# Decay tiles from a transpose and two-row products, block inverses on 128 partitions, four splits left out, and a new order

## The chip, the cores and the metric

One Trainium2 chip, one of its cores. The time is the device time of one execution in microseconds (us); the kernel before takes 655.69 us, the median of 3 runs (655.58 to 655.97).

## What is computed

The reference is one decoder layer on 512 rows of 1024 float32 numbers. A modulated normalisation feeds one input projection; half of its columns go to a gated delta rule with 4 heads, half to a sparse attention; both meet in an output projection, and a gated MLP with a short convolution follows. The change lies in the gated delta rule, in what leads up to it, and in the order of everything:

```python
gc = jnp.cumsum(g, axis=-1)
decay = jnp.exp(jnp.where(incl, gc[..., :, None] - gc[..., None, :], NEG_INF))
a_mat = jnp.where(strict, jnp.einsum('bhncd,bhnsd->bhncs', k_beta, k) * decay, 0.0)
t_mat = lax.linalg.triangular_solve(eye + a_mat, jnp.broadcast_to(eye, a_mat.shape),
                                    left_side=True, lower=True, unit_diagonal=True)
...
u = t_mat @ (v * beta[..., None])
w = t_mat @ (k_beta * jnp.exp(gc)[..., None])
...
xs = tuple(jnp.moveaxis(t, 2, 0) for t in (u, w, q_dec, k_dec, attn_intra, g_last))
_, o = lax.scan(step, state0, xs)
```

The reference takes chunks of 64 rows; the kernel takes 4 chunks of 128, with the same result.

## The kernel before, in words

The program is written as a long list of operations, in sections: filling matmuls at the start (`warm`, as many as `IDLE` says), normalisation and modulation of the input, the first projection (`g0`, over 8 slices k of the contraction), small gate projections (`small`), convolutions, norms, the delta rule, the attention, the output projection, and the MLP (`up1`, `down`). The first of the delta rule's sections are `prep`, `blocks`, `invert` and `scan`. While the list is written, `record` only notes each operation with the tiles that it touches. Then `emit` issues all of them, some 7,000, in an order that a packed table in the file (`ORDER`) fixes, and a second table (`CHOICE`) says for those that either ScalarE (ACT) or VectorE (DVE) could do which of them does it. Each engine works through its own part of the list in that order, and waits where an operand isn't ready or a buffer not free. Buffers are taken from fixed classes as the list goes: 90 of 512 columns (S), 4 of 1024 columns for raw loads (R), 32 small ones (s), 8 PSUM banks (P), and kept ones (C). So the table sets which buffer is reused when, too. All instructions are issued by one line of `emit`, which is why the profile shows one line for all of them: L280 before, L273 after.

Matrix products are done in float32 accuracy by splitting each operand into a rounded high part and a low part (`split`), and by three passes: high x high, high x low, low x high. Weights come from DRAM as raw loads on the sync engine's queue (SP); some of the accumulating transfers go through GpSimd's (POOL).

For the delta rule, `prep(t)` makes for each of the 4 chunks the tile exp(decay) for all 4 heads at once: VectorE multiplies the log decays by a triangle (`tg`), splits the product, and TensorE sums a mask (`negTr`) and the two halves over 128 rows with a matrix of ones (`onesr`) into the PSUM bank `pb`; ScalarE takes the exponential. The strictly triangular matrix times decay, `uu`, goes to DRAM (`du`).

`blocks` fetches the 64 diagonal blocks of 32x32 from there (4 chunks x 4 heads x 4 blocks), one block on each of 64 partitions, in two halves of 16 rows (`uh`), and inverts all of them at once by forward substitution: in 31 steps VectorE multiplies a column of the block by a row of the inverse so far, and subtracts that from the rows below. The inverse lies in two halves too (`xh`), so most steps take three instructions. It is written to DRAM (`dx`), and `invert(t)` fetches it back with one row a partition (`xc`), spreads it to a block diagonal matrix (`xx`), and joins blocks of 32 to 64 and to 128 by products on TensorE.

`norm2` normalises the input of the MLP, and splits it into `h2h` and `h2l`, some columns of which nobody reads.

## Time and profile before

| | us |
|---|---|
| median of 3 runs | 655.69 |
| span of the profiled execution | 653.6 |
| TensorE (PE) busy, 4,170 instructions | 647.5 |
| VectorE (DVE) busy | 623.9 |
| ScalarE (ACT) busy | 471.8 |
| GpSimd (POOL) busy | 135.5 |
| the 16 DMA engines, mean | 202 GB/s over the span |

The profiled execution has no time of its own beside its span; the median of the runs is 2.1 us above it. The table shows busy time, which counts an instruction from its start to its end; those of one engine overlap, so the price of one in a full queue is the distance from start to start.

### The profile page before, as it was taken

The page shows a single profiled execution, that of the slowest core. Times are in us where ns is not written, and L with a number is a line of the kernel's source. Part 1 is how long each engine was busy: PE and PEld are TensorE (multiplying, and loading weights), DVE is VectorE, ACT ScalarE, POOL GpSimd, SP SyncE. Part 2 cuts the span into 40 slices and gives each one's busy share as a digit, 9 for nine tenths or more (in the row PEclk, how much of TensorE's full clock was granted, in tenths as well). Part 3 has the DMA queues.
Part 4 walks back from the last instruction along what each step waited for, and adds up shares of the span by engine and source line. Part 5 has one row for each costly group of instructions (what it writes and reads, how often), then busy time and mean ns, then how long its engine had stood idle before and what let it go on. Part 6 is the DMA issues. An engine that isn't in the chain of part 4 may idle for free.

```text
span 653.6 us, 12682 instructions
## 1 busy us (share of the span) xinstructions
PE 647.5 (99%) x4170; PEld 584.0 (89%) x4170; DVE 623.9 (95%) x1542; ACT 471.8 (72%) x1184; POOL 135.5 (21%) x158
## 2 busy tenths in 40 slices
PE   9999999999999999999999999999999999999997
PEld 9886888888988889888899999999999998888886
DVE  7999999989999999999999999999989999999997
ACT  6666996355679998746875665766677899998850
POOL 0000100010100003302222523334234432344400
PEclk9999999999999999999999999999999999999999
DMA  9997656656524689985777998999899999999913
GB/s 321 393 357 260 193 184 191 195 136 171 136 66 131 195 275 243 230 255 128 174 157 195 174 178 191 218 218 197 204 226 211 202 235 268 274 182 205 152 30 130
DMA packets 67484, 132.03 MB, mean 202 GB/s; under 512 B 11333, under 2 KB 11989, under 8 KB 67417
## 3 DMA queue, kind: packets, MB, share of 16 engines
q1 hardware_dynamic: 45352, 91.07, 41.6%
q0 software_dynamic: 22064, 40.14, 37.1%
q8 instruction: 33, 0.54, 0.3%
q14 instruction: 35, 0.28, 0.1%
HBM read 109.42 MB, written 3.41 MB: 173 GB/s over the span
## 4 chain that ended last, share of the span: by engine, by line
PE 89%; DVE 5%; DMA 4%; issue 1%; ACT 1%; SPq 0%; DVEq 0%
PE P L280 89%; DVE S L280 4%; DMA R<-in_wg_dram 2%; DMA S<-in_adat_dram 2%; DMA S<-in_x_dram 1%; ACT S L280 1%; SPq L280 0%; DVE C L280 0%; DVE s L280 0%; DVEq L280 0%
## 5 line engine op out<-in xcount | busy, mean ns | idle before, releaser
L280 PE MATMUL P<-S,S 128*128 128x256 f32 (+4 forms) x3675 | 604.1, 324 | 0.0
L280 PEld LDWEIGHTS P<-S,S 128*128 128x128 f32 (+2 forms) x3675 | 522.0, 190 | 53.4 <-issue 0.4
L280 DVE TENSOR_TENSOR S<-S,S 128x512 fp32r<-128x512 f32 (+14 forms) x489 | 245.0, 545 | 6.0 <-ACT S L280 2.0
L280 ACT ACTIVATE S<-S 128x512 fp32r<-128x512 f32 (+3 forms) x378 | 187.5, 548 | 41.0 <-DVE S L280 28.6
L280 ACT ACTIVATE S<-P 128x256 f32<-128x256 f32 (+4 forms) x208 | 83.4, 420 | 64.6 <-PE P L280 61.3
L280 POOL DMA_DIRECT2D S<-R x46 | 43.3, 971 | 289.2 <-DVE S L280 158.6
L280 ACT ACTIVATE S<-R 128x512 fp32r<-128x512 f32 (+2 forms) x153 | 85.9, 583 | 18.7 <-DMA R<-in_wn_dram 6.0
L280 POOL DMA_DIRECT2D S<-in_wu_dram x66 | 62.8, 1017 | 134.7 <-DVE S L280 97.9
L280 DVE SCALAR_TENSOR_TENSOR S<-S,C,S 128x511 f32<-128x511 f32 (+2 forms) x116 | 85.0, 744 | 0.8 <-ACT S L280 0.6
L280 DVE TENSOR_TENSOR S<-P,S 128x256 f32<-128x256 f32 (+3 forms) x124 | 65.3, 535 | 7.6 <-PE P L280 5.0
L280 DVE TENSOR_TENSOR S<-R,S 128x512 fp32r<-128x512 f32 (+2 forms) x100 | 57.6, 588 | 0.4 <-ACT S L280 0.3
L280 ACT ACTIVATE S<-S,C 128x512 f32<-128x512 f32 (+1 forms) x70 | 44.9, 657 | 15.6 <-DVE S L280 7.7
L280 PE MATMUL P<-C,S 128*128 128x128 f32 (+2 forms) x285 | 51.1, 268 | 0.6 <-DVE S L280 0.5
L280 PEld LDWEIGHTS P<-C,S 128*128 128x128 f32 (+1 forms) x285 | 36.8, 145 | 7.5 <-DVE S L280 0.9
L280 DVE SCALAR_TENSOR_TENSOR S<-S,S 128x512 f32<-128x512 f32 x62 | 40.9, 685 | 1.0 <-DMA S<-in_adat_dram 1.0
L280 ACT ACTIVATE S<-S,s 128x128 f32<-128x128 f32 (+4 forms) x75 | 34.3, 479 | 4.2 <-DVE s L280 4.1
L280 ACT ACTIVATE S<-P,C 128x128 f32<-128x128 f32 (+1 forms) x71 | 28.0, 436 | 10.9 <-PE P L280 8.1
L280 POOL DMA_DIRECT2D S<-S x24 | 21.1, 892 | 51.0 <-ACT S L280 46.2
L280 DVE SCALAR_TENSOR_TENSOR S<-P,C,S 128x511 f32<-128x511 f32 (+3 forms) x48 | 29.9, 643 | 0.2
L280 ACT ACTIVATE S<-P,C,C 128x128 f32<-128x128 f32 (+2 forms) x35 | 16.6, 530 | 9.4 <-DVE C L280 8.3
L280 DVE TENSOR_TENSOR S<-S,P 128x256 f32<-128x256 f32 (+1 forms) x39 | 18.6, 477 | 0.6 <-PE P L280 0.4
L280 PE MATMUL P<-S 128*128 128x256 f32 (+1 forms) x96 | 17.3, 322 | 1.2 <-DVE S L280 1.2
(79 smaller groups left out, 296.8 us busy)
## 6 DMA issues: line engine op xcount, KB each, us to landing
S<-in_wu_dram POOLq DMA_DIRECT2D x66, 256.0 KB, 5.7
S<-in_adat_dram SPq DMA_DIRECT2D x64, 256.0 KB
S<-R POOLq DMA_DIRECT2D x46, 256.0 KB, 5.7
S<-in_wu_dram SPq DMA_DIRECT2D x44, 256.0 KB
R<-in_wu_dram SPq DMA_DIRECT2D x22, 512.0 KB
S<-in_wd_dram SPq DMA_DIRECT2D x44, 256.0 KB
S<-in_adag_dram SPq DMA_DIRECT2D x32, 256.0 KB
R<-in_wn_dram SPq DMA_DIRECT2D x12, 512.0 KB
```

Source lines behind the costliest of these rows:

```text
L280: getattr(engines[eng], method)(*map(place, args), **{k: place(v) for k, v in kw.items()})
```

## The change

- `prep`: the log decays, which lie as columns, are turned into rows once, by one transpose on TensorE into the bank `pgr`; the 16 rows are split, and two small transfers on GpSimd's queue lay them out as `grow`, with the high and the low row of each chunk on two neighbouring partitions. The second and third pass into `pb` become one, over two rows. The triangle product, its split and their buffers go. This adds the chunk's row to the exponent without the triangle; the column's part is the exponential's bias, as before, and the mask still closes the upper half.
- `blocks`: the inverse's even columns lie on partitions 0 to 63 and its odd ones on 64 to 127. The blocks are copied to the upper 64 partitions by two more transfers, each step takes one product and one difference over half as many columns, and the two memsets go. The result is written to `dx` with even and odd columns interleaved again by rows of 16, `2048x1x16`, twice; `invert` reads it as before and spreads it in two instructions instead of one.
- `norm2`: four splits whose result nobody reads are left out (t = 3, kk up to 3).
- `IDLE` is 57 instead of 64, the constant `eye16` is replaced by `eye2` (256 columns more), and a function that nothing calls, `up_mm`, is gone.
- `ORDER` and `CHOICE` are new for the whole program.

```diff
-IDLE = 64
+IDLE = 57
...
+    pgr, gcf = bank("pgr"), u("gcf", F32R, (P, 256))[:16]
+    T.transpose(pgr[:16, :P], gc, ident)
+    split(pgr[:16, :P], gcf[:, :P], gcf[:, P:])
+    grow = u("grow", F32R)
+    for i in range(2):
+        G.dma_start(bass.AP(tensor=grow.tensor, offset=grow.offset + i * 512, ap=[[32 * 512, 4], [P, 4], [1, P]]),
+                    gcf[:, i * P:i * P + P])
+
     def prep(t):
         tok = toks[t]
         pb = bank("pb")
-        tg, gh_, gl_ = u("tg"), u("gh", F32R), u("gl", F32R)
-        V.tensor_mul(h4(tg), rows4(cs("triu")), bc(g[:, t * 4:t * 4 + 4]))
-        split(tg, gh_, gl_)
         T.matmul(h4(pb), identr, rows4(negTr), start=True, stop=False)
-        T.matmul(pb, onesr, gh_, start=False, stop=False)
-        T.matmul(pb, onesr, gl_, start=False, stop=True)
+        T.matmul(pb, onesr[32 * t:32 * t + 2, :], grow[32 * t:32 * t + 2, :], start=False, stop=True)
...
-        uh = [u("ub", shape=(P, 16, 32))[:64] for _ in range(2)]
-        xh = [u("xb", shape=(P, 16, 32))[:64] for _ in range(2)]
+        uh = [u("ub", shape=(P, 16, 32)) for _ in range(2)]
+        xb = u("xb", shape=(P, 32, 16))
...
-        tm = u("r")[:64]
-        eye = cs("eye16")[:64].rearrange("p (i j) -> p i j", i=16)
         for i in range(2):
-            V.memset(xh[i], 0.0)
-            V.tensor_copy(xh[i][:, :, i * 16:i * 16 + 16], eye)
+            Q.dma_start(uh[i][64:], uh[i][:64])
+        tm = u("r")
+        V.tensor_copy(xb, cs("eye2").rearrange("p (i j) -> p i j", i=32))
         for j in range(31):
-            n, m = 31 - j, j + 1
+            n, m = 31 - j, j // 2 + 1
...
-            top = max(0, 15 - j)
-            if top:
-                V.tensor_sub(xh[0][:, j + 1:16, 0:m], xh[0][:, j + 1:16, 0:m], tv[:, :top, :])
-            lo = max(0, j - 15)
-            V.tensor_sub(xh[1][:, lo:16, 0:m], xh[1][:, lo:16, 0:m], tv[:, top:, :])
-        for i in range(2):
-            Q.dma_start(dx[:, i * 512:(i + 1) * 512], xh[i].rearrange("p i j -> p (i j)"))
+            V.tensor_sub(xb[:, j + 1:32, 0:m], xb[:, j + 1:32, 0:m], tv)
+        for s in range(2):
+            Q.dma_start(dx.rearrange("p (i s j) -> p i s j", i=32, s=2)[:, :, s, :], xb[s * 64:s * 64 + 64])
...
-                if t % 2:
+                if t == 1 or t == 3 and kk > 3:
...
+c-nQFcbHVw()DYf?w%QjAtOl6QF6{mybL+RfaIW(gXA0)BuZ2yBN8M_lB^OWNJer7LCG*o=svr?-<kV9-(T;0dE^e==j>g(YSpT>`t*p@k^P!X>dIby7aoW=
...
```

What the new order moves is shown at three places. The first is TensorE's beginning. Before, its queue begins as follows; S_79 is the filler's operand and P_141 its bank, C_117 the identity, and the passes of 128x1 are sums over partitions:

```order
L280 MATMUL P_141<-S_79 128x256 x29
L280 MATMUL P_171<-C_117,C_115 128x128 x4
L280 MATMUL P_180<-C_117,C_115 128x128 x4
L280 MATMUL P_141<-S_79 128x256 x7
L280 MATMUL P_198<-C_117,S_83 128x128
L280 MATMUL P_141<-S_79 128x256 x2
L280 MATMUL P_211<-C_117,S_83 128x128
L280 MATMUL P_141<-S_79 128x256 x7
L280 MATMUL P_222<-C_115,S_213 128x1
L280 MATMUL P_141<-S_79 128x256
L280 MATMUL P_222<-C_115,S_213 128x1
```

After, S_85 and P_103 are the filler's:

```order
L273 MATMUL P_103<-S_85 128x256 x13
L273 MATMUL P_117<-C_90,C_81 128x128
L273 MATMUL P_119<-C_90,C_81 128x128 x2
L273 MATMUL P_117<-C_90,C_81 128x128 x2
L273 MATMUL P_119<-C_90,C_81 128x128 x2
L273 MATMUL P_117<-C_90,C_81 128x128
L273 MATMUL P_103<-S_85 128x256 x14
L273 MATMUL P_189<-C_90,S_83 128x128
L273 MATMUL P_191<-C_90,S_83 128x128
L273 MATMUL P_197<-C_90,S_83 128x128
L273 MATMUL P_103<-S_85 128x256 x11
L273 MATMUL P_197<-C_90,S_96 128x128
```

A run of 29 fillers has become one of 13, ahead of the eight small passes that make the modulation's columns; the transposes of the input (C_90 against S) and the sums over partitions stand in larger groups. Behind these rows, 39 passes of the projection's first slice stand ahead of the second slice before, and 42 after.

The second place is the load queue SP, around the second slice of the projection's weights (`in_wg_dram`, the second in each list). Before:

```order
L280 DMA S_200<-in_adat_dram 128x512
L280 DMA S_213<-in_adat_dram 128x512
L280 DMA R_259<-in_wg_dram 128x896
L280 DMA S_263<-in_adat_dram 128x512
L280 DMA S_280<-in_adat_dram 128x512
L280 DMA S_283<-in_adat_dram 128x512
L280 DMA S_285<-in_adat_dram 128x512
L280 DMA S_301<-in_adat_dram 128x512
L280 DMA S_303<-in_adat_dram 128x512
L280 DMA S_317<-in_adat_dram 128x512
L280 DMA S_321<-in_adat_dram 128x512
L280 DMA R_326<-in_wg_dram 128x896
```

After:

```order
L273 DMA S_173<-in_adat_dram 128x512
L273 DMA S_201<-in_adat_dram 128x512
L273 DMA S_206<-in_adat_dram 128x512
L273 DMA S_221<-in_adat_dram 128x512
L273 DMA S_237<-in_adat_dram 128x512
L273 DMA S_241<-in_adat_dram 128x512
L273 DMA S_251<-in_adat_dram 128x512
L273 DMA S_258<-in_adat_dram 128x512
L273 DMA S_269<-in_adat_dram 128x512
L273 DMA S_292<-in_ws_dram 128x160
L273 DMA S_302<-in_adat_dram 128x512
L273 DMA R_312<-in_wg_dram 128x896
```

The second slice has moved from place 21 of the queue to place 23: one more load of modulation weights (`in_adat_dram`, 256 KB each) and the small gate projection's weights (`in_ws_dram`, 80 KB) stand ahead of it.

The third place is SP and VectorE around the way of the inverses through DRAM. SP before:

```order
L280 DMA dx<-S_89 64x512
L280 DMA R_1901<-in_wn_dram 128x1024
L280 DMA S_1910<-in_cst_dram 128x195
L280 DMA S_1952<-in_adat_dram 128x512
L280 DMA S_1962<-in_adat_dram 128x512
L280 DMA dx<-S_87 64x512
L280 DMA S_2006<-dx 128x4x32
L280 DMA S_2008<-in_adat_dram 128x512
L280 DMA S_2056<-dx 128x4x32
```

SP after:

```order
L273 DMA dx<-S_1187 2048x1x16
L273 DMA S_1798<-in_adat_dram 128x512
L273 DMA R_1811<-in_wt_dram 128x1024
L273 DMA dx<-S_1187 2048x1x16
L273 DMA S_1861<-in_adat_dram 128x512
L273 DMA S_1869<-dx 128x4x32
L273 DMA S_1876<-dx 128x4x32
L273 DMA R_1878<-in_wn_dram 128x1024
L273 DMA S_1888<-in_adat_dram 128x512
L273 DMA S_1901<-dx 128x4x32
```

VectorE after, the last rows ahead of and with the first spreading of the inverse (S_1869 is `xc`):

```order
L273 SCALAR_TENSOR_TENSOR S_1823,s_1822<-S_1295,S_245 128x512
L273 TENSOR_TENSOR S_1796<-S_1796,C_79 128x512
L273 SCALAR_TENSOR_TENSOR S_1830,s_1829<-S_1263,S_245 128x512
L273 SCALAR_TENSOR_TENSOR S_1836,s_1835<-S_1686,S_245 128x512
L273 SCALAR_TENSOR_TENSOR S_1838,s_1822<-S_1251,S_255 128x512
L273 TENSOR_SCALAR C_1841<-C_1646 128x16
L273 SCALAR_TENSOR_TENSOR S_1844,s_1843<-S_955,S_255 128x512
L273 SCALAR_TENSOR_TENSOR S_1854,s_1853<-S_1189,S_245 128x512
L273 SCALAR_TENSOR_TENSOR S_1866,s_1843<-S_971,S_245 128x512
L273 TENSOR_TENSOR S_1874<-R_1693,S_1757 128x512
L273 SCALAR_TENSOR_TENSOR S_1886,s_1885<-S_1713,S_255 128x512
L273 TENSOR_TENSOR S_1890<-S_1869,S_1764 128x256 x2
```

The second write of `dx` now stands behind a raw load (R_1811, 512 KB), which goes into a buffer that VectorE frees with the difference from R_1288, four rows ahead of the first of these; ten rows of the modulation's products, and four others of that length or shorter, stand between that and the inverse's first multiply.

More of the change, by code (lines that the diff above doesn't have):

```diff
@@ new lines @@
+Vx*01Q}6%(w?D-sOqPfDjQ{VyBIGAkZT$b=^~*YqmP9?ML*=#>mKS<iGfH_msV_90{Hqzb=5Ng`DJ7SD`G4+VWR^VE(`t3D4AR{4k48#5S@geNe^mNw9o9GU
+vFy;4l288Btnx;S%kNrAE@>+HO{>UTeZx<EWeR^^(h^csZgTDS|FdFmX&@8z5B*h!@=7YH$h&L!sku1vP_sxBCkknOXSW+Bxuu4z)JEK!U0!Jl?oKP!<e>JH
+g8#>PMvB!(8Ya<_M@q;QR(7PVY}RWUB=0`SLN+dQ!i?+{CjDf$Zq@u!UCyabCdx8R)Q4JHZs=H|m`euV=~a!8GMu9TwFv4lEh6vv`5!9rA$L91kL5bqPD2hW
+%K+*zMn-Yk#WI8y<5V1DpXe(+tE1!;wF@Idj(j8Sx%*#D;L5j}To%bvP0hM5G?P5xweD2<5xc+Sl;PB{Skl>CJx?B{NG~#xN#gan2BZg>_sJ*nonBOz>n>^q
+d89d{gKX3TT9CVLX*S6$2_VDOIQCL@dB#2mh&9Mh*EA<_Hk8tGmW=#L?ms4Txv0*2Fck%=?o-?6WF`gK59fY|Rqv6{>l&}Mc_*kRwG?YaN@3oK1|!ADUM4Vk
@@ new lines @@
+?A(D|eujq{&7EB&Id^*s{h+os*>JztbdkJ6yUmq{yzV{gsqD=_l+74sNGm4iKzgVPY#N}#hH4L?I(w47fgDNRpAttL>{Aw>as))ZC&n3gqRPbk4h7p1%<R=H
+bZi#qvK}XfzTlvt+^`Ky<)q&V^47{tBt9+boJCvLK-DiNmyXoIo4iHG&O~Wv=G8Z>l8YXWB(pc@o}*fgNs?Sn;L0p}ejzROzleRQE68w79Lqvp{|A-Yj*3i!
+7oQPBP8`7u`n{4I(C_Krp=jLsRCk0-rRVOV!@7g%j`9Q7FQsnT=|azUX5e%$;r@lX2D~)IdtAYX&H$(L=;yR(%fGadMwwue*9b@r>UV*Yc;ByWB28d{5oE-H
+Yop+Uy{zW_=1p#9!+Pn)-*NDL4ltP=6`w*bgWU461m>zQ-fw=yqB6$1b)D)kU3WMsOirn%ek(|JeZpO#q|fM{kdv!gmu}wSj&gi5$?fi-INg!Xef6H#7Lj4@
+Am@q3=rt7636LIzg1_PYu8W>Ti5BL>b;)ccP`cD@??j9DtoO9G)(0?UaY+vA4F#D^>GcG<z)5<_JX}04mW@|j^?u{W!$~9xDLm=>0{;&$X8o@
@@ L181 @@
 """
 CHOICE = """
[L183 to L185 removed]
+c-qBLu?@mN3_L%H6j6OiLGdLeBfKI8$Ox2-VMQ#E4Ja9fk`WjM;`e_(37`~6oRnC$le6y(M0gay7C(Vm_Sr6k3qZ}hyAGky=L2}0T3~g%&+A5ZvNG}7l7sQ7
+M;Q~xY>Z|`C^##@L-T#=97E{3!)x#<R?9ZBP|2Jx9ko&~bu&z;<n4f3O`TZl-B<tRcP7q7`CbYIp``4p--K-(d^Dy?J4h`%gu`$jokhZzZ8-JP3kgj{q=L<>
+RVcWT6U)GOf3N@G2{9iOVg
@@ L739, in invert @@
         xx, yy = u("X"), u("Y")
-        V.tensor_mul(xx.rearrange("p (h b j) -> p h b j", h=4, b=4),
-                     xc.rearrange("p h (o j) -> p h o j", o=1).to_broadcast([P, 4, 4, 32]),
-                     cs("bd").rearrange("p (o b q) -> p o b q", o=1, q=1).to_broadcast([P, 4, 4, 32]))
+        xc = xc.rearrange("p h (s j) -> p h s j", s=2)
+        for s in range(2):
+            V.tensor_mul(xx.rearrange("p (h b j s) -> p h b j s", h=4, b=4, s=2)[:, :, :, :, s],
+                         xc[:, :, s, :].rearrange("p h (o j) -> p h o j", o=1).to_broadcast([P, 4, 4, 16]),
+                         cs("bd").rearrange("p (o b q) -> p o b q", o=1, q=1).to_broadcast([P, 4, 4, 16]))
         V.transpose(yy, xx)
@@ L1128, in hybrid_block @@
     act = [None] * NF
-    def up_mm(ps, wc, a, b):
-        for k in range(KT):
-            mm3(ps[:, a:b], cols(wc[k // 4], hs[k % 4]), (h2h[k][:, a:b], h2l[k][:, a:b]), k == 0, k == KT - 1)
     def conv3(ps, f, s):
```

229 lines of the change are left out of this document (104 added, 125 removed).

## The prediction

> **What bounds the kernel now.** I read the page's head and its chain first, then the chain in order of time.
>
> ```profile
> span 653.6 us, 12682 instructions
> PE 89%; DVE 5%; DMA 4%; issue 1%; ACT 1%; SPq 0%; DVEq 0%
> ```
>
> ```profile
> 6.75 5.92 DMA S<-in_adat_dram
> 12.69 6.93 DMA R<-in_wg_dram
> 19.64 5.87 DMA S<-in_adat_dram
> ...
> 60.99 0.76 DVE S L280
> 61.80 181.31 PE P L280 x1028
> ...
> 646.15 2.57 DVE S L280 x5
> 648.74 1.11 DVE S L280 x2
> 649.88 0.42 DVE S L280
> ```
>
> The columns are start, length, and what ran. Up to about 32 us the chain follows loads, then VectorE to 61.8; from there it is TensorE's own queue almost to the end, and a tail of about 7 us on VectorE and the store that the change leaves as it is. The span is 653.6 and the median of the runs 655.69, so 2.1 us lie around the span; I add them back at the end.
>
> How full TensorE is, stage by stage, is in the table of windows (busy time and starts of each engine, granted clock, DMA share, GB/s):
>
> ```profile
> core 0: us, PE busy (x) PEld busy (x) DVE busy (x) ACT busy (x) POOL busy (x), PEclk, DMA share, GB/s
> 6.05:16.03 9.98, 9.98 (x87) 9.87 (x87) 9.24 (x50) 8.13 (x20) 0.00 (x0) 1.00 1.03 384
> 16.03:20.70 4.67, 4.67 (x41) 4.67 (x40) 4.67 (x17) 3.73 (x8) 0.00 (x0) 1.00 1.04 391
> 20.70:62.00 41.30, 40.75 (x191) 31.32 (x190) 40.48 (x107) 24.96 (x42) 0.00 (x0) 1.00 0.91 334
> 116.80:143.70 26.90, 26.90 (x132) 22.20 (x132) 24.98 (x88) 13.89 (x31) 2.58 (x3) 1.00 0.56 163
> 340.00:380.00 40.00, 40.00 (x334) 39.91 (x334) 39.14 (x79) 27.72 (x58) 14.43 (x16) 1.00 0.89 190
> 560.00:600.00 40.00, 40.00 (x178) 33.14 (x177) 40.00 (x92) 36.89 (x83) 15.75 (x18) 1.00 0.98 203
> ```
>
> Busy time and length agree in every row but one: between 20.70 and 62.00 TensorE is idle for 0.55 us. So time taken from VectorE or ScalarE is worth nothing by itself: only TensorE instructions that go, and waits of TensorE, count. Two prices come from here: 40.00/334 = 0.120 us from start to start where nearly all matmuls have 256 columns, and 40.00/178 = 0.225 us where nearly all have 512. The start is different: up to 20.7 us the DMA engines are full (share 1.03 to 1.04, 384 to 391 GB/s), and TensorE is kept busy with idle-filling matmuls.
>
> **The change, part by part.**
>
> *The start: seven filling matmuls fewer, new load order: +0.35 us.* The fillers are worth 7 x 0.120 = 0.84 us, but they stand where TensorE waits for data. The first projection matmul is at 16.03:
>
> ```profile
> 16.03 1.24 PE L280 MATMUL P<-S,S 128*128 128x256 f32 x9
> 61.00 0.27 PE L280 MATMUL P<-C,S 128*128 128x128 f32 x1
> 61.80 0.44 PE L280 MATMUL P<-C,S 40*128 40x40 f32 x4 [0.53 <-DVE S L280]
> ```
>
> It needs the first quarter of the normalised input, and in both orders the last load for that is the 14th, behind the same 3.7 MB; so I keep 16.0. Next is the second slice of the projection weights. It was issued at 12.69 and landed 6.93 later at 19.62, and its first use was at 20.70. In the new order it is load 23 instead of 21, with 262 + 82 KB more ahead: 0.344 MB at 391 GB/s is 0.88 us, so it lands at 20.50. ScalarE splits half a slice in 0.53 us (two in 1.05):
>
> ```profile
> 19.64 1.05 ACT L280 ACTIVATE S<-R 128x384 fp32r<-128x384 f32 x2
> ```
>
> That gives 21.03. TensorE itself has 42 first-slice matmuls ahead now (39 before): 16.03 + 42 x 0.120 = 21.07. Both say 21.05, +0.35. Bounds: -0.5, if filler and loads give way together, and +0.9, if the load's whole delay counts.
>
> *TensorE's work behind that point: -1.15 us.* Three of the 256-column matmuls moved ahead of the point, -0.36. Each of the four decay tiles takes two passes of 512 columns instead of three, -4 x 0.225 = -0.90; that the second contracts two rows instead of 128 I price at nothing, since fewer rows have not made passes shorter here:
>
> ```profile
> L280 PE MATMUL P<-S,S 128*128 128x512 f32 x1257 | 319.0, 399 | 0.0
> L280 PE MATMUL P<-S,S 128*40 128x512 f32 x8 | 3.1, 393 | 0.0
> L280 PE MATMUL P<-C,S 40*128 40x40 f32 x4 | 0.4, 236 | 0.5 <-DVE S L280 0.5
> ```
>
> The transpose that makes the rows adds one pass like the last row's, 0.44/4 = 0.11. The new order also changes how often fp32 and rounded passes alternate; no row prices that, and the 0.120 and 0.225 contain it as it was, so it stays at 0, with 0.5 us to either side.
>
> *The wait at 61: -0.6 us.* From 61.00 to 61.80 TensorE starts nothing, where such a pass takes 0.11: 0.69 us lost to VectorE, which was behind (40.48 of 41.30 us busy in that window). Its two memsets are gone, the small gate projection's weights are loaded ahead of the second slice now, and that projection's transposes stand elsewhere. What is late next are the evictions of the gate and norm work at 72 to 78; I leave 0.1 us for them. Bounds: -0.7 and +0.5, a new wait as long as the old.
>
> *The block inverses and the split of the rows on VectorE and ScalarE: 0.* The inverse loop is these rows:
>
> ```profile
> L280 DVE TENSOR_TENSOR S<-S,S 64x192 f32<-64x192 f32 (+23 forms) x78 | 22.4, 301 | 1.9
> ```
>
> 93 small instructions become 62, with half the elements a partition. At 301 ns as a latency, and less from start to start, some 9 us leave VectorE. They lie beside TensorE's 26.90 busy of 26.90 us in that window, so nothing is gained; and were the loop not shorter at all, nothing is lost. The same holds for four splits of 128x256 that nobody reads.
>
> *The inverses' way through DRAM: 0, if pieces of 64 bytes are cheap.* The result was written as rows of 2 KB, and is now written as 2 x 2048 pieces of 64 bytes, then read as before. The trace has pieces of 128 bytes in the reads (512 for 64 KB):
>
> ```profile
> 134.39 0.51 SPq L280 DMA_DIRECT2D dx<-S  x1
> 134.99 0.53 SPq L280 DMA_DIRECT2D R<-in_wn_dram  x1
> ...
> 149.63 0.39 SPq L280 DMA_DIRECT2D S<-dx  x1
> ```
>
> ```profile
> 136.40:137.40 1.00, 1.00 (x6) 0.74 (x5) 0.90 (x4) 0.44 (x1) 0.00 (x0) 1.00 0.76 135
> 150.60:151.30 0.70, 0.70 (x4) 0.58 (x4) 0.70 (x4) 0.52 (x2) 0.00 (x0) 1.00 0.78 117
> ```
>
> 0.78 x 0.70 us x 16 engines / 512 is at most 17 ns a piece, and the read is in by about 151.5, 1.9 after its issue. The write and the weight load behind it were through by about 137.4, so a write takes at most 3.0. In the new order the second write stands behind a 512 KB load into a buffer that VectorE frees; from there to the inverse's first multiply VectorE has 14 more rows, one short and 13 of the length of these two, some 0.61 from start to start, together 8.1 us:
>
> ```profile
> 152.85 0.69 DVE L280 SCALAR_TENSOR_TENSOR S<-S,S 128x512 f32<-128x512 f32 x1
> ...
> 153.47 0.69 DVE L280 SCALAR_TENSOR_TENSOR S<-S,S 128x512 f32<-128x512 f32 x1
> ```
>
> The transfers need three issues of 0.4, 3.0 for the write, 1.8 for its pieces (128 an engine x 17 ns, less the 0.34 that 128 KB took), and 1.9 for the read: 7.9 us. TensorE has 48 passes of 512 columns ahead of the inverse, 10.8 us from the matmul that frees that buffer, and VectorE's chain reaches it after 0.4 + 0.6 + 8.1 + 0.8 = 9.9. So about 1 us is free on both sides; up to some 25 ns a piece it costs nothing. The upper end is a piece as dear as one of 2 KB, 85 ns at 24 GB/s an engine: 128 x (85 - 25) = 7.7 us. I take 0, since the 17 ns row is the nearest.
>
> *The rows' way to the decay tiles: 0.* Two small transfers from GpSimd now feed them, behind a 256 KB accumulation in its queue:
>
> ```profile
> S<-R POOLq DMA_DIRECT2D x46, 256.0 KB, 5.7
> C<-in_par_dram POOLq DMA_DIRECT2D x1, 24.0 KB, 3.3
> ```
>
> Issues of about 0.9 each and 3.3 to 5.7 to land make 5 to 8 us behind the split; between the transpose and the first decay tile TensorE's order has about 10 us of other matmuls. Bounds 0 and +2.
>
> **Sum:** 0.35 - 1.15 - 0.6 = -1.4. 653.6 - 1.4 = 652.2, and with the 2.1 around it 654.3.
>
> **Rivals.** A difference of 0.2%, 1.3 us, is about what can be told from no change.
>
> *The gain is larger.* The start gives back 0.5 instead of taking 0.35, and the alternation is worth 0.5: -1.15 - 0.6 - 1.0 gives 652.9. For it: 4 us of fillers stand ahead of 16.03 in all. Against it: the DMA engines are full there.
>
> *Nothing to measure.* The second slice's delay counts in full (+0.9) and the wait at 61 comes back elsewhere (-0.1): 655.3. For it: VectorE stays the second busiest engine (40.48 of 41.30), and any order of 7,000 rows has places as tight as the one removed. Against it: VectorE has less to do throughout.
>
> *A written piece costs twice a read one.* At 34 ns TensorE waits (34 - 25) x 128 = 1.2 us ahead of the first inverse: 655.5. For it: no write below 2 KB stands in this trace. Against it: nothing but the 17 ns of the reads. The Trainium skill's page "DMA: Bandwidth & Descriptors" (section "Specifications") says that transfers below 512 bytes are read, modified and written back; the reads of 128 bytes to SBUF here show no such price, and for writes to DRAM by that rule the time would be this rival's, or more.
>
> *Slower, by the 64-byte writes.* TensorE stands right behind the first inverse, with the 1 us of margin worked out above. From 25 ns a piece on, each 10 ns cost 1.3 us; slower than before by 1.3 needs 46 ns, and 85 ns gives 662. For it: the chain is serial, and TensorE waits there directly. Against it: 17 ns for reads twice the size.
>
> *It does not relieve VectorE,* because small instructions have a floor. Then the loop still falls by its 31 missing instructions, and TensorE does not notice: 654.3 as well.
>
> **How the numbers follow.** Forecast 654.3 with its near neighbours 0.54 (two thirds of that below 654.4, since the sum's open ends reach further down than up), which holds the loop that relieves nobody; larger gain 0.10; nothing to measure 0.16; doubled pieces 0.06; slower by writes 0.10; by the rows' transfers or a tight place in the attention stage 0.04. Faster by over 0.2%: 0.36 + 0.10 = 0.46. Within 0.2%: 0.18 + 0.16 + 0.06 = 0.40. Slower: 0.14. The range leaves out the far half of the larger gain and most of the slow cases: 652.8 to 657.0.
>
> **What would show it.** Right: the first projection matmul at about 16.0, the first of the second slice at about 21.0; no wait above 0.3 us at 61; TensorE with 4,160 starts and no idle time from 62 to the tail; the loop on VectorE near 13 us with TensorE full beside it; the first inverse's passes without a wait. Wrong: a wait of TensorE ahead of that inverse that ends with the read from DRAM, a projection start away from 16.0, or waits on the decay tiles that end with GpSimd's transfers.

## The result, and the profile after

The changed kernel takes 661.78 us, the median of 6 runs (658.99 to 664.50); the kernel before took 655.83 beside it (655.52 to 656.45, 6 runs). The ratio is 1.0095, with a 95% interval of 1.0076 to 1.0115: slower, outside the range of the prediction and on its other side. The profiled execution took 660.93, 2.1 us more than its span. The page's head, its chain, and the chain in order of time (start, length, what ran):

```profile
span 658.8 us, 12659 instructions
PE 89%; DMA 4%; ACT 3%; DVE 2%; issue 1%; SPq 0%; ACTq 0%; DVEq 0%; POOLq 0%
```

```profile
17.11 44.46 PE P L273 x230
...
67.60 1.28 ACT L273
68.90 0.64 ACT S L273
69.58 78.69 PE P L273 x401
148.28 289.64 PE P L273 x2021
...
440.30 7.23 DMA S<-R
447.57 37.04 PE P L273 x306
```

VectorE has gone from 5% of the chain to 2%, as the change meant it to. But the first projection matmul stands at 17.11 instead of 16.03, TensorE's queue is broken at 68, where before it was not, and from 440 on, in the MLP, DMAs are in the chain, which ran through there on TensorE alone before (start and length again):

```profile
246.62 399.50 PE P L280 x2764
```

None of the three stands at the decay tiles or the inverses, where the diff edits the computation; the diff also takes seven fillers from the start. Whether the new order made these places is what the experiments ask. How TensorE and the DMA engines stood in the MLP, before (first row) and after, is in the table of windows (busy time and starts of TensorE, granted clock, DMA share, GB/s):

```profile
430.00:560.00 130.00, 130.00 (x1024) 1.00 0.99 226
```

```profile
430.00:560.00 130.00, 127.52 (x1011) 1.00 0.96 210
560.00:640.00 80.00, 80.00 (x357) 1.00 0.86 180
```

TensorE stood still for 2.48 us there. The DMA engines were nearly full in both kernels (0.99 and 0.96), but after moved (226 - 210) x 130 = 2.1 MB less, and had to move it later (180 GB/s behind 560, where before had 151). ScalarE's waits in that stretch (us in total, times, longest) show what is late; the same view of before has no such row:

```profile
ACT S L273 <- DMA R<-in_wu_dram: 5.9, 2, 4.4
ACT S L273 <- DMA S<-in_wd_dram: 2.4, 3, 1.5
```

### The profile page after: what moved, and what is told of

Read it like the earlier page. It is cut to its first block, busy times and chain, and to the rows that moved or that the text cites. A ratio compares the mean times of both kernels' runs of the same rounds, so it can differ in the third digit from the quotient of the medians.

```text
span 658.8 us, 12659 instructions
## 1 busy us (share of the span) xinstructions
PE 649.1 (99%) x4160; PEld 582.0 (88%) x4160; DVE 618.6 (94%) x1542; ACT 468.5 (71%) x1158; POOL 138.9 (21%) x160
## 4 chain that ended last, share of the span: by engine, by line
PE 89%; DMA 4%; ACT 3%; DVE 2%; issue 1%; SPq 0%; ACTq 0%; DVEq 0%; POOLq 0%
PE P L273 89%; ACT S L273 3%; DVE S L273 2%; DMA R<-in_wu_dram 1%; DMA S<-R 1%; DMA S<-in_wd_dram 1%; DMA S<-in_x_dram 1%; DVE s L273 0%; ACT L273 0%; SPq L273 0%; ACT s L273 0%; ACT C L273 0%; ACTq L273 0%; DVEq L273 0%; POOLq L273 0%
## 5 line engine op out<-in xcount | busy, mean ns | idle before, releaser
L273 PE MATMUL P<-S,S 128*128 128x256 f32 (+3 forms) x3675 | 605.6, 323 | 2.6 <-ACT S L273 2.1
L273 PEld LDWEIGHTS P<-S,S 128*128 128x128 f32 (+1 forms) x3675 | 524.2, 189 | 58.8 <-ACT S L273 4.6
L273 DVE TENSOR_TENSOR S<-S,S 128x512 fp32r<-128x512 f32 (+9 forms) x470 | 234.6, 542 | 8.4 <-PE P L273 2.3
L273 ACT ACTIVATE S<-S 128x512 fp32r<-128x512 f32 (+3 forms) x357 | 177.4, 547 | 47.7 <-DVE S L273 29.4
L273 ACT ACTIVATE S<-P 128x256 f32<-128x256 f32 (+5 forms) x205 | 81.5, 418 | 69.6 <-PE P L273 67.4
L273 ACT ACTIVATE S<-R 128x512 fp32r<-128x512 f32 (+2 forms) x162 | 90.1, 587 | 26.7 <-PE P L273 7.3
L273 POOL DMA_DIRECT2D S<-R x46 | 44.5, 1031 | 282.1 <-PE P L273 94.9
L273 POOL DMA_DIRECT2D S<-in_wu_dram x66 | 62.6, 1018 | 138.8 <-DVE S L273 109.1
L273 DVE SCALAR_TENSOR_TENSOR S<-S,C,S 128x511 f32<-128x511 f32 (+2 forms) x116 | 84.8, 743 | 1.8 <-ACT S L273 1.7
L273 DVE TENSOR_TENSOR S<-P,S 128x256 f32<-128x256 f32 (+4 forms) x125 | 65.5, 532 | 10.8 <-PE P L273 7.6
L273 DVE TENSOR_TENSOR S<-R,S 128x512 fp32r<-128x512 f32 (+2 forms) x100 | 57.3, 587 | 0.1
L273 PE MATMUL P<-C,S 128*128 128x128 f32 (+3 forms) x285 | 50.2, 271 | 2.3 <-DVE s L273 1.3
L273 ACT ACTIVATE S<-S,C 128x512 f32<-128x512 f32 (+1 forms) x65 | 42.7, 677 | 6.7 <-DVE S L273 3.5
L273 PEld LDWEIGHTS P<-C,S 128*128 128x128 f32 (+1 forms) x285 | 35.2, 145 | 9.8 <-ACT S L273 2.1
L273 DVE SCALAR_TENSOR_TENSOR S<-S,S 128x512 f32<-128x512 f32 x62 | 40.8, 685 | 0.1
L273 POOL DMA_DIRECT2D S<-S x26 | 22.8, 915 | 46.3 <-ACT S L273 38.3
L273 ACT ACTIVATE S<-P,C 128x128 f32<-128x128 f32 (+1 forms) x71 | 26.7, 437 | 8.0 <-PE P L273 7.9
L273 DVE SCALAR_TENSOR_TENSOR S<-P,C,S 128x511 f32<-128x511 f32 (+3 forms) x48 | 29.8, 642 | 2.1 <-ACT S L273 1.6
L273 ACT ACTIVATE S<-S,s 128x128 f32<-128x128 f32 (+4 forms) x63 | 29.1, 482 | 0.9 <-DVE s L273 0.9
L273 ACT ACTIVATE S<-P,C,C 128x128 f32<-128x128 f32 (+2 forms) x35 | 16.4, 531 | 8.7 <-DVE C L273 5.1
L273 POOL DMA_DIRECT2D S<-in_wd_dram x17 | 17.5, 1508 | 15.4 <-DVE S L273 15.4
L273 DVE TENSOR_TENSOR S<-S,P 128x256 f32<-128x256 f32 (+1 forms) x39 | 18.5, 476 | 2.3 <-PE P L273 1.9
```

Source lines behind the costliest of these rows:

```text
L273: getattr(engines[eng], method)(*map(place, args), **{k: place(v) for k, v in kw.items()})
```

## Experiments

Each ratio is to the kernel before, run beside it, with its 95% interval in brackets. All operations are issued by one line of `emit`, whose number differs from kernel to kernel (L250, L255, L273). Where only the tables change, the edit is written as a formula: lists of operations in order, each with the engine that its table gave it.

### The MLP's order

**e1_mlp_old_order**: the old order from TensorE's first `up1` matmul on, which is operation 3099 of the new order and 3251 of the old one.

```diff
-order = after
+order = after[:3099] + [o for o in before if o not in after[:3099]]
```

> The changed kernel up to TensorE's first matmul of the MLP; from there on every operation in the order (and on the engine) that it had before. Theory A (the new order asks for the MLP's weights too late; the waits of TensorE at 447, 474, 499, 526 and 549 us, about 4 us in the profiled run, come from that): these waits go, 656.0 to 657.8, and the runs lie within 1 us of one another. Rival B (the waits have another cause, in the changed computation or in the DMA engines' own variation): 660 or more, runs spread over several us.

657.47 (656.49 to 658.52, 10 runs), 1.0028 [1.0018, 1.0037].

**e2_old_with_new_mlp_order**: the reverse, in the kernel before.

```diff
-order = before
+order = before[:3251] + [o for o in after if o not in before[:3251]]
```

> The kernel before, with its own order up to the first matmul of the MLP and the new order from there on. Theory A: 659 to 662 and a spread of several us from the MLP's order alone. Rival B: 655.5 to 656.5, like before.

663.44 (662.31 to 664.55, 4 runs), 1.0120 [1.0105, 1.0135].

So the MLP's part of the new order costs 661.78 - 657.47 = 4.3 us in the changed kernel, and 663.44 - 655.63 = 7.8 in the old one. In the changed kernel that is most of the loss, with no edit of the code in it. The 7.8 lies above what was expected, and not all of it is the MLP's: where the two orders are joined, between 321 and 368, TensorE has five waits of 1.5 us together that neither kernel has, and the moved part also holds 73 passes of the output projection. To see why the MLP's order costs time, both kernels ran with less work for the DMA engines.

**e7_new_short_acc** and **e8_old_short_acc** (the same edit in the kernel before). An accumulating transfer adds only the first quarter of its columns, so sums stay incomplete and the result is not the reference's; the operations and their order stay.

```diff
-        G.dma_start(lo, src, accum_op=OP.add)
+        m = lo.shape[-1] // 4
+        G.dma_start(lo[:, :m], src[:, :m], accum_op=OP.add)
...
-                G.dma_start(src, then, accum_op=OP.add)
+                m = src.shape[-1] // 4
+                G.dma_start(src[:, :m], then[:, :m], accum_op=OP.add)
```

> The changed kernel with its own order, but the accumulating transfers of the weights' splits and of the MLP's weight combinations move only the first quarter of their columns (the rest of the low halves and of the combined weights stays incomplete). Theory that the MLP's waits come from DMA engines that are full there, so that a late transfer can't be caught up: the share of the DMA engines from 430 to 560 falls from 0.95 to 0.7 or less, TensorE's waits at 447, 499 and 550 are gone, and the time is 657.5 or less, about 2 us over e8_old_short_acc. Rival that VectorE's and ScalarE's places in the new order make the splits late: the waits stay, and the distance to e8_old_short_acc stays 5 us or more.

> The kernel before with the same shortened accumulating transfers (the rest of the low halves and of the combined weights stays incomplete). Both theories: TensorE waits for none of these transfers in before, so 655.4 to 655.8; it is the partner of e7_new_short_acc.

e7: 657.43 (656.49 to 659.19), 1.0033 [1.0020, 1.0046]. e8: 655.21, 0.9996 [0.9987, 1.0005]. The same window of e7:

```profile
430.00:560.00 130.00, 130.00 (x1031) 1.00 0.60 141
```

With the DMA share at 0.60 TensorE has no wait left in 130 us, in the very order that cost 2.48 there; the time falls by 4.4, as much as e1 gave, and before is indifferent to the edit. VectorE's and ScalarE's places were the same, so it isn't they. One load shows both halves of the cause. In the changed kernel TensorE waits 1.50 us at 501.08 for the split of a weight load that was issued at 492.36 and took 7.69 us to land. In e1 the same load is issued 9.8 us earlier, at 482.58, and in e7 as late as in the changed kernel, at 492.15; in neither does TensorE wait for it. So the stretch has next to no spare DMA time, and an order that issues its loads later did not catch up there.

### The decay tiles

**e3_rows_128** (e1 with this edit)

```diff
+    sel = u("sel", F32R)
...
-        T.matmul(pb, onesr[32 * t:32 * t + 2, :], grow[32 * t:32 * t + 2, :], start=False, stop=True)
+        T.matmul(pb, sel[:, hs[t]], grow, start=False, stop=True)
...
+    V.memset(grow.bitcast(F32), 0.0)
+    V.memset(sel.bitcast(F32), 0.0)
+    for t in range(NT):
+        V.memset(sel.bitcast(F32)[32 * t:32 * t + 2, hs[t]], 1.0)
```

> As e1, but the decay pass contracts 128 rows instead of 2: a matrix that picks the two rows (ones there, zeros elsewhere) against the row tile with zeros around; six memsets more on VectorE at the start. Theory C (a pass over 2 rows costs 0.42 us instead of 0.225 and slows the pass ahead of it and the one behind by 0.10 and 0.11, 0.4 us each time): 1.6 us less than e1, and all passes around it 0.23 us apart. Rival D (these passes are slow for another reason: their operand comes late, or the bank is switched): as e1 within 0.4 us.

656.84 (654.81 to 658.50, 10 runs), 1.0018 [1.0007, 1.0029]: 0.6 less than e1 where 1.6 was expected, and the intervals overlap; the spans of the profiled executions are 654.8 and 653.0. TensorE's rows of the changed kernel (start, length, form as rows contracted * columns, count):

```profile
88.44 0.49 PE L273 MATMUL P<-S,C 2*128 2x512 f32 x1
88.86 0.51 PE L273 MATMUL P<-S,S 128*128 128x512 f32 x1
89.20 0.40 PE L273 MATMUL P<-C,C 128*128 128x512 f32 x1
89.53 0.49 PE L273 MATMUL P<-S,C 2*128 2x512 f32 x1
89.95 2.09 PE L273 MATMUL P<-S,S 128*128 128x512 f32 x12
```

and of e3:

```profile
92.93 0.40 PE L255 MATMUL P<-C,C 128*128 128x512 f32 x1
93.16 4.06 PE L255 MATMUL P<-S,S 128*128 128x512 f32 x17
```

A two-row pass takes 88.86 - 88.44 = 0.42 from start to start, the pass behind it 89.20 - 88.86 = 0.34 and the one ahead of the next 0.33, where 4.06 us for 17 shows passes of 128 rows at 0.23. So by these rows each visit to two rows costs some 0.2 + 0.1 + 0.1 = 0.4 us; four make 1.6, nearly twice what the pass left out saved. The times show less, 0.6 here and 1.0 below (e5 against e6), and neither is clear of its intervals. The Trainium skill ("TensorEngine Tiling (Array Packing)", section "Key Properties") says that a change of the tiling mode drains TensorE. Whether a pass over two rows is such a change no run shows; if it is, these rows are its price.

**e5_old_order** and **e6_old_order_rows_128** (e5 with e3's edit)

```diff
-order = after
+order = [o for o in before if o in after], new operations behind what they need
```

> All edits of the change in the code (transpose and two-row products, block inverses on 128 partitions, four splits fewer, 57 fillers), but every operation at the place that it had in the order of before, and on the same engine; the new operations stand behind what they need, and the products into pb of chunks 2, 3 and 0 some 5 to 7 us later, since the rows have to arrive first. Theory that the order is the loss, and that each two-row pass costs 0.42 us and 0.10 and 0.11 more in the passes beside it: 4 x (0.63 - 2 x 0.227) = +0.7 and a transpose +0.1, so 656.4. Rival, the price of the prediction (a pass less is 0.225 less, two rows cost nothing): 654.9. Rival that the loss is in the edits themselves (the inverses' 64-byte pieces or the rows' transfers): 658 or more, with a wait of TensorE ahead of the first inverse or of a decay tile.

> As e5_old_order, but the second pass into pb contracts 128 rows: a matrix that has ones in the chunk's two rows and nothing elsewhere selects them (five memsets on VectorE at the start, and one that clears the rows' buffer). Theory that a pass over two rows is what costs: each decay tile is one pass of 0.227 shorter than before and the transpose adds 0.1, so -0.8 against before, 654.8, and 1.6 less than e5_old_order. Rival that the passes' price comes from elsewhere (the small transfers, the mask's pass): within 0.3 of e5_old_order.

e5: 658.72 (658.14 to 660.86, 5 runs), 1.0050 [1.0036, 1.0064]; e6: 657.72, 1.0032 [1.0020, 1.0045]. The step from two rows to 128 is worth 1.0 here. The times lie 2.3 and 2.9 us above what the theory of the order had (656.4 and 654.8), and e5 lies where its last rival put it, with a wait at a decay tile. But it wasn't the edits in themselves: e11 below has e6's edits with the new operations in other places, without the loss. Here they stood badly. In e5 TensorE waits 1.23 us, for ScalarE, which is behind an exponential of a decay tile that waits for the late rows:

```profile
97.59 0.49 PE L250 MATMUL P<-S,C 2*128 2x512 f32 x1
99.31 0.51 PE L250 MATMUL P<-S,S 128*128 128x512 f32 x1 [1.23 <-ACT S L250]
```

### The start, and the wait at 68

**e4_start_old_order**, where `head` is what before issues up to its 40th projection matmul.

```diff
-order = e1
+order = head + [o for o in e1 if o not in head]
```

> As e1, but everything up to the first matmul of the projection's second slice in the order before (57 fillers). Theory E (the start lost time because the input's rows are loaded in another order, so that the normalisation begins 2 us later): first projection matmul at 16.0 and second slice at 20.7 to 21.0 as before, 1.2 to 1.6 us less than e1. Rival F (the weights' load sets it): the second slice at 22.3 as in the changed kernel, same time as e1.

657.58 (657.18 to 658.12, 6 runs), 1.0031 [1.0019, 1.0044], no better than e1. The start itself did move, as the theory of the loads' order had it: the first projection matmul stands at 16.44 (16.79 in e1), and the second slice starts at 21.1 (22.2). But where the two orders are joined there are new waits for ScalarE, 0.63 at 24.3 and 0.65 at 54.4, which take it back. As to the time of the start this run decides nothing; it comes up again below.

**e9_table_early** (e3 with one operation more on ScalarE)

```diff
+    S.activation(small("warm", 1), pr("c")[:, 0:1], AF.Silu)
```

> e3_rows_128 with one operation more: a Silu of one column on ScalarE, right behind its last operation ahead of the wait at 68. ScalarE then fetches the table that it needs next while it would stand idle, instead of when VectorE's result is there (1.28 us at 67.6 in the changed kernel, with TensorE waiting 0.89 for what follows). Theory that this fetch makes the wait: the wait at 68 is below 0.2, the fetch stands at 66 to 67, and the time is 0.7 to 0.9 less than e3_rows_128 had, 656.0. Rival that VectorE is what is late there: the wait stays at 0.6 or more and the time at 656.8.

657.19 (654.80 to 660.04, 12 runs), 1.0024 [1.0009, 1.0039]. The wait at 68 of the changed kernel, ScalarE and then TensorE:

```profile
67.60 1.28 ACT L273 ACT_TABLE_LOAD   x1 [0.96 <-DVE S L273]
68.90 1.15 ACT L273 ACTIVATE S<-S 128x512 f32<-128x512 f32 x2
```

```profile
69.58 0.44 PE L273 MATMUL P<-C,S 128*128 128x128 f32 x2 [0.73 <-ACT S L273]
```

and ScalarE in e9:

```profile
66.63 1.28 ACT L255 ACT_TABLE_LOAD   x1
67.92 0.20 ACT L255 ACTIVATE s<-C 128x1 f32<-128x1 f32 x1
68.03 1.14 ACT L255 ACTIVATE S<-S 128x512 f32<-128x512 f32 x2
```

The fetch fills the 0.96 us that ScalarE had idled, Silu comes 0.87 earlier, and TensorE's wait is gone. The mechanism is shown. The time did not follow: 0.7 to 0.9 less than e3 was expected, and 0.35 more was measured, which is within the noise. The profiled execution (659.71, the second slowest of the 12) has a new wait, of 2.93 us ahead of the first inverse; whether the faster ones have it too isn't shown:

```profile
144.26 1.31 PE L255 MATMUL P<-S,S 128*128 128x128 f32 x7
148.50 3.80 PE L255 MATMUL P<-S,S 128*128 128x128 f32 x17 [2.93 <-ACT S L255]
```

```profile
147.33 0.63 ACT L255 ACTIVATE S<-R 128x512 fp32r<-128x512 f32 x1 [4.38 <-DMA R<-in_wn_dram]
```

TensorE waits for ScalarE, and ScalarE for a weight load. What this wait cost is more than its length, as the windows of e9 show (granted clock in the column behind the starts):

```profile
146.00:148.00 2.00, 0.00 (x0) 1.00 0.80 147
148.00:150.00 2.00, 1.50 (x9) 0.75 0.10 21
150.00:152.00 2.00, 2.00 (x10) 0.50 0.34 124
```

Behind the pause TensorE's clock is at 0.50 from 149.0 to 152.4, 3.4 us, which makes about 1.7 us more (an estimate: half the work of that time). The Trainium skill ("TensorE: Matmul & The Clock Gate", section "What's actually happening") has a clock that falls to half after an idle window of about 3.4 us, and rises again after about 3.4 us of work. The length of the slow stretch agrees; but a pause of 2.93 us was enough for the fall here, and in e17 below pauses of at most 0.70 us went ahead of one.

### The old order, mended

**e10_old_order_mended** (e6 with new places for the new operations) and **e11_old_order_placed**, whose difference to e10 in SyncE's queue is

```diff
 L250 DMA S_1835<-in_adat_dram 128x512
+L250 DMA R_1874<-in_wn_dram 128x1024
+L250 DMA S_1883<-in_cst_dram 128x451
 L250 DMA dx<-S_1227 2048x1x16 x2
-L250 DMA R_1876<-in_wn_dram 128x1024
-L250 DMA S_1885<-in_cst_dram 128x451
```

> e6_old_order_rows_128 with the new operations put elsewhere: the rows' split 6 places later on VectorE (TensorE stood 0.7 us behind it at 82.7), the products into pb of chunks 0, 2 and 3 and their exponentials 2 to 3 us earlier (TensorE stood 1.4 us at 96.3 behind a weight split that was queued behind a late exponential on ScalarE), and the last steps of the inverse with their transfers where before had its first transfer. Theory that the edits are worth 0.8 once no order costs them anything, and that the start with 57 fillers takes about 0.5 of it: 655.2 to 655.6, with no wait of TensorE over 0.3 from 80 to 160. Rival that the way of the rows through GpSimd's queue is too long for this place: a wait of 1 us or more for ScalarE or a transfer between 88 and 100 again, and 656.5 or more.

> e10_old_order_mended with the inverses' two transfers to DRAM issued behind the next two loads of SyncE's queue instead of ahead of them (there the first load stood behind them until 142.4, and TensorE waited 2.8 us at 147 for what is split from it), and the rows' split one place later still on VectorE, the mask's pass next to the rows' pass. TensorE ran 0.44 to 0.46 us behind before at 100 to 145 in e10_old_order_mended, so without that wait the time is 655.6 plus 0.2 to 0.5: 655.8 to 656.1. Rival that the two transfers are late in any place, since both wait for the last step where before had the first half done at 134: a wait of 1 us or more ahead of the first inverse, and 657 or more.

e10: 658.73 (657.05 to 660.23, 6 runs), 1.0047 [1.0032, 1.0062], where 655.2 to 655.6 was expected: the waits at 82 and 96 shrank to 0.2 and nothing, but SyncE stood at the two writes until 140.67, and the weight load behind them came late; ScalarE waited 8.24 us for it, and TensorE 2.76 behind that:

```profile
148.14 1.15 ACT L250 ACTIVATE S<-R 128x512 fp32r<-128x512 f32 x2 [8.24 <-DMA R<-in_wn_dram]
```

```profile
150.58 1.65 PE L250 MATMUL P<-S,S 128*128 128x512 f32 x7 [2.76 <-DVE S L250]
```

e11, with two loads ahead of the writes: 654.97 (653.81 to 657.08, 12 runs), 0.9992 [0.9982, 1.0001], 3.8 less than e10. Two loads stand ahead of the two writes there, and some of TensorE's passes for the decay tiles stand otherwise too, so the 3.8 is the price of these places together; the wait of 2.76 is one part of it.

### The pieces of 64 bytes

**e12_long_pieces** (e9 with this edit)

```diff
-            Q.dma_start(dx.rearrange("p (i s j) -> p i s j", i=32, s=2)[:, :, s, :], xb[s * 64:s * 64 + 64])
+            Q.dma_start(dx[:, s * 512:(s + 1) * 512], xb[s * 64:s * 64 + 64].rearrange("p i j -> p (i j)"))
```

> e9_table_early, but the inverses go to DRAM in rows of 2 KB instead of pieces of 64 bytes (even and odd columns then lie one behind the other there, and are read back in that order, so the inverse matrices are not those of the reference). Theory of the prediction that the pieces cost nothing: the time stays within 0.6 of e9_table_early, 656.6 to 657.8, with the same spread of about 5 us and waits for a weight load ahead of the first inverse in some executions. Rival that the pieces hold up the transfers behind them: 655.8 or less, a spread of 2 us, and no wait at 145.

655.35 (654.25 to 656.92, 12 runs), 1.0000 [0.9991, 1.0008]: 1.8 less than e9, so the prediction's theory that the small pieces cost no time falls. (The edit writes rows of 2 KB with even and odd columns apart and leaves the read as it was, so the result is not the reference's.) SyncE's queue in e9 (start, length of the issue):

```profile
130.62 0.54 SPq L255 DMA_DIRECT2D dx<-S  x1
132.70 2.06 SPq L255 DMA_DIRECT2D S<-in_adat_dram  x1
136.54 0.93 SPq L255 DMA_DIRECT2D S<-dx  x2
```

and in e12:

```profile
130.74 0.47 SPq L255 DMA_DIRECT2D dx<-S  x1
132.81 0.34 SPq L255 DMA_DIRECT2D S<-in_adat_dram  x1
134.74 2.18 SPq L255 DMA_DIRECT2D S<-dx  x2
```

The load behind a write of 2,048 pieces takes 2.06 us to issue instead of 0.34, and the read of the inverse can be issued 136.54 - 130.62 = 5.9 us behind the write instead of 4.0. How that becomes time stays open. The next load behind the reads is issued only 0.55 us later than in e12 (137.56 against 137.01), and the weight load of e9's wait only 0.5 later (139.64 against 139.13). e3 has the same small pieces and issues that load at 139.53, and TensorE does not wait there; nor does it at the first inverse in the profiled executions of e1 and of the changed kernel. So the price is shown by the medians, with a spread of 5.2 us in e9 against 2.7 in e12, and not by one wait.

Nor are the pieces dear in themselves. In the changed kernel 1,360 of them lie in 131.6 to 132.6 us, at a DMA share of 0.811: 0.811 x 1.0 us x 16 engines / 1360 is 9.5 ns each, less than the 17 ns of the prediction.

**e13_read_pieces** (e9), **e14_old_order_read_pieces** (e11) and **e15_new_read_pieces** (the changed kernel), each with

```diff
-            Q.dma_start(dx.rearrange("p (i s j) -> p i s j", i=32, s=2)[:, :, s, :], xb[s * 64:s * 64 + 64])
+            Q.dma_start(bass.AP(tensor=dx.tensor, offset=dx.offset + s * 2048, ap=[[4096, 16], [512, 4], [1, 512]]),
+                        xb[s * 64:s * 64 + 64].rearrange("p i j -> p (i j)"))
...
-        Q.dma_start(xc, bass.AP(tensor=dx.tensor, offset=dx.offset + t * 16 * 1024,
-                                ap=[[32, P], [4 * 1024, 4], [1, 32]]))
+        Q.dma_start(xc.rearrange("p h (s j) -> p (h s) j", s=2),
+                    bass.AP(tensor=dx.tensor, offset=dx.offset + t * 16 * 1024,
+                            ap=[[16, P], [2048, 8], [1, 16]]))
```

> e9_table_early, with the inverses written to DRAM in rows of 2 KB (even and odd columns apart), and fetched back in pieces of 64 bytes instead of 128, 1024 for a chunk instead of 512; the result is that of the reference. Theory that what costs is the writing in small pieces: 655.4, as e12_long_pieces, with its spread of 2 to 3 us. Rival that any small piece costs, read or written: 656.6 or more, as e9_table_early or above, and waits ahead of the first inverse.

> e11_old_order_placed with the same two edits (2 KB rows written, 64-byte pieces read). Theory that writing in small pieces costs where the transfers behind them are needed at once: in this order the inverse had no wait in the profiled execution, so at most 0.3 less than e11_old_order_placed, 654.7, with less spread than its 3.3 us. Rival that the longer read, 64 bytes a piece, is late now: a wait of TensorE ahead of the first inverse and 655.5 or more.

> The changed kernel in its own order with the same two edits alone (2 KB rows written, 64-byte pieces read). Theory that the small written pieces cost about 1.8 in this order, whatever else is late: 660.0. Rival that the MLP's waits and the one at 68 hide or replace it: 661.2 or more.

e13: 655.62 (654.64 to 656.65, 11 runs), 1.0001 [0.9993, 1.0010]. e14: 654.55 (653.81 to 655.60, 11 runs), 0.9985 [0.9977, 0.9994]. e15: 659.04 (658.14 to 663.14, 6 runs), 1.0066 [1.0045, 1.0087]. So it is the writing in small pieces that costs; reading 64 bytes at a time, twice as many pieces as the change had, shows no cost. In the changed kernel the edit gives 661.78 - 659.04 = 2.7 us, more than the 1.8 expected. That this is the pieces' price isn't shown: the intervals overlap, and e15's execution (661.35) has a wait of 0.88 ahead of the inverse, while the MLP's wait at 501 is gone. e14 is the one version whose interval shows it faster than both kernels, by 0.15%: the old order with all edits of the change but the split into two-row passes and the small written pieces.

### Where the fillers stand

**e16_fillers_first** (e13) and **e17_new_fillers_first** (the changed kernel), each with nine fillers moved:

```diff
-L255 MATMUL P_111<-S_85 128x256 x13
+L255 MATMUL P_111<-S_85 128x256 x22
...
-L255 MATMUL P_111<-S_85 128x256 x14
+L255 MATMUL P_111<-S_85 128x256 x5
```

> e13_read_pieces with the same 57 fillers, nine of which are moved from TensorE's second block to its first, so that 22 instead of 13 stand ahead of the first products with the identity. Theory that TensorE runs at half pace (0.213 us a filler instead of 0.119) until it has been busy for some 4 us without a pause, and that 13 fillers end after 3.1 us: in executions in which it then waits for the identity the slow pace begins anew, and up to 2 us of the start are lost. Then fillers at 0.213 end before 6 us in the profiled execution, the first projection matmul stands at 16.6 or earlier, and the time is 0.5 to 1.2 below e13_read_pieces: 654.4 to 655.1, with a spread under 1.5. Rival that the start waits for loads whatever TensorE's pace is: 655.3 to 655.9.

> The changed kernel in its own order with nothing but the same move of nine fillers. Theory of the pace: up to 1 us less where the slow pace came back, so 660.6 to 661.2 beside 661.8, as far as the MLP's spread lets it be seen, and no filler at 0.213 after 6 us. Rival: no change beyond the spread, 661.5 or more.

e16: 654.60 (654.12 to 656.87, 11 runs), 0.9992 [0.9983, 1.0000], 1.0 less than e13. e17: 658.66 (656.54 to 659.67, 6 runs), 1.0045 [1.0031, 1.0059], 3.1 less than the changed kernel. TensorE's beginning in e13:

```profile
1.19 3.14 PE L255 MATMUL P<-S 128*128 128x256 f32 x13 [1.19 <-DVE S L255]
5.01 3.78 PE L255 MATMUL P<-C,C 128*128 128x128 f32 x16 [0.68 <-ACT C L255]
```

and in e16:

```profile
1.19 5.06 PE L255 MATMUL P<-S 128*128 128x256 f32 x22 [1.19 <-DVE S L255]
6.05 2.35 PE L255 MATMUL P<-C,C 128*128 128x128 f32 x16
```

The nine fillers more took 5.06 - 3.14 = 1.92 us, 0.21 each, in place of the 0.120 that the prediction had from before's later ones. In e13 TensorE pauses for 0.68 behind its 13, and the products behind run slow once more (3.78 instead of 2.35 for the same 16). The first projection matmul comes at 16.50 in e16, and at 17.77 in e13. In the profiled execution of the changed kernel itself, which also has 13 ahead, the slow pace did not come back; TensorE loses its time further on, where it waits for VectorE:

```profile
4.30 2.06 PE L273 MATMUL P<-C,C 128*128 128x128 f32 x16
9.33 0.55 PE L273 MATMUL P<-C,S 128*128 128x128 f32 x3 [1.31 <-DVE s L273]
```

VectorE's first statistic of the input starts at 6.32 there, behind a load of an input row, and at 3.52 in before. So the normalisation starts later in the new order of the loads, and the fillers have no part in that.

e17 came out 2 us below what was expected of it, and its profile doesn't show the start as the reason: a pause of 0.70 at 8.25 is left, the clock is at 0.50 from 15 to 17 (below), the first projection matmul is at 17.73, later than in the changed kernel, and TensorE is 0.5 us behind the changed kernel at 70. It is 1.6 ahead at 548, with the MLP's wait at 501 gone.

```profile
15.00:17.00 2.00, 2.00 (x11) 0.50 1.07 390
```

So the fillers account well for the 1.0 us of e16, though the intervals of e13 and e16 overlap, and not for the 3.1 of e17. The MLP's wait at 501 is gone in e15 and e17, which have the MLP's new order; whether it varies from execution to execution, or with what stands far ahead of it, one profile of each can't tell.

## Why the prediction was wrong, point by point

What the points below say of TensorE's lead is read from rows of before

```profile
213.99 0.40 PE L280 MATMUL P<-S,S 128*68 128x512 f32 x1
...
638.84 10.54 PE L280 MATMUL P<-S,S 128*128 128x512 f32 x57
```

and the same operations in e14 (the first of them stands beside before's row at 61.80):

```profile
61.67 0.44 PE L250 MATMUL P<-C,S 40*128 40x40 f32 x4 [0.51 <-DVE S L250]
...
213.21 0.40 PE L250 MATMUL P<-S,S 128*68 128x512 f32 x1
...
638.76 9.87 PE L250 MATMUL P<-S,S 128*128 128x512 f32 x54
```

- **The step that failed first is one that isn't in the sum.** That "any order of 7,000 rows has places as tight as the one removed" stood among the rivals, where it gave back 0.5 us, the gain of one wait. The MLP, whose DMA engines stand at 0.99 for 130 us, got no term, though the prediction quoted a share of 0.98 for 560 to 600 beside TensorE's 40.00 of 40.00. It is the largest loss: 4.3 us (e1), since its loads are issued later where the DMA engines have nothing to spare (e7).
- **"the last load for that is the 14th, behind the same 3.7 MB; so I keep 16.0"**, of the first projection matmul. It stood at 17.11. The sum counted bytes, and not which rows of the input come first: VectorE's first statistic waits for its row until 6.32, and TensorE 1.31 us for VectorE at 9.33; with the old start the matmul stands at 16.44 (e4, e1's 16.79). The sum also took fillers for padding at 0.120 each, where the first 22 took 0.23 (5.06 us, e16); where the slow pace comes back (e13, 17.77) nine fillers moved give 16.50 (e16). The term was +0.35, with the second slice at 21.05; this matmul is 17.11 - 16.03 = 1.1 late, and the second slice starts at 22.30, 1.6 later than before's 20.70. How this divides between loads and fillers isn't separated.
- **"that the second contracts two rows instead of 128 I price at nothing, since fewer rows have not made passes shorter here"**: the step rested on a misread row: in `128*40 128x512` the 128 is the rows contracted, and 40 the columns. No row of before had so few rows contracted in a 512 pass. The term was -0.90. By the rows it is about -0.9 + 1.6 = +0.7; by the times, which show 0.6 to 1.0 for the two rows (e3, and e6 against e5), about 0. With 128 rows it is right: between two operations that both kernels have, TensorE in e14 gains (213.99 - 213.21) - (61.80 - 61.67) = 0.65 on before, for 0.79 forecast (-0.90 + 0.11).
- **"The wait at 61: -0.6 us."** It went, as forecast, and another came at 68, with 0.73 in its row for the 0.53 of before's at 61.80, so a little beyond the bound, "a new wait as long as the old". "What are late next are the evictions of the gate and norm work" was the wrong candidate: it is a table fetch of 1.28 us on ScalarE (13 fetches after, 7 before). e9 shows it.
- **"The inverses' way through DRAM: 0, if pieces of 64 bytes are cheap ... about 1 us is free on both sides."** The condition held, and the zero did not follow from it: at 9.5 ns a piece is cheap, and the small writes cost 1.6 to 1.8 us on e9's base all the same (e12, e13). In the changed kernel their price isn't separated (e15). The margin was worked out for the inverse alone; the issue behind the write, which takes 2.06 instead of 0.34, and the loads queued behind the read were not followed. Which wait makes the loss stays open. The rivals by written pieces named the right operation, but by prices of 34, 46 and 85 ns that no piece had.
- **"The block inverses and the split of the rows on VectorE and ScalarE: 0."** Right. Up to the first of these rows at 213 VectorE is busy for 191.2 us in e14 and 201.0 in before, 9.8 less for the "some 9 us" forecast. TensorE is 0.78 ahead of before at 213 and (638.84 + 10.54) - (638.76 + 9.87) = 0.75 ahead at its last matmul, which is the gain of the passes and no more: less work on VectorE was worth nothing. Behind that matmul e14's execution is another 0.6 us shorter (3.6 instead of 4.2), though the prediction kept the tail as it was; no run shows why.
- **"The rows' way to the decay tiles: 0."** Right in the new order, which has the room; in the old one e5 and e10 had them where ScalarE or a load was late, and e11 shows places without a loss.

Taken away one on top of the other, the causes lead from the changed kernel back to about the time of before: 661.78, 657.47 (MLP's order, e1), 656.84 (128 rows, e3), 657.19 (table, e9), 655.62 (pieces, e13), 654.60 (fillers, e16). Only the first step is clear of the intervals by itself; the pieces' step is at their edge, and the table fetch shows no gain in the median.

## What to carry to other kernels

Where a change brings a new order, the order is the change: price first the stretch whose DMA engines are full, since there a later issue was not caught up here, and only then the instructions that went. A margin holds for a whole queue, so follow whatever stands behind the waiting transfer to the engine that needs it. And read a form's two numbers in their right sense before a price is taken from it: a small contraction was not free here.
